# Score products inside the chunks of two gated scans: four places of the TensorE array and a PSUM bank per head

## Chip, cores, metric

The kernel runs on one core of one Trainium2 chip. The metric is the device time of one execution in microseconds. The kernel before was run three times: 878.19, 876.57 and 876.63 us, median 876.63. The profile comes from an execution of its own, which took 878.09 us; the span that it shows, from the first to the last instruction, is 876.2 us.

## What is computed

One layer of an encoder trunk over 512 positions and 1024 channels: a modulated RMS norm, one projection into all branches, three token mixers in parallel (differential attention with 4 heads, the HGRN2 scan with 4 heads of 64 channels, the GLA scan with 4 heads of 32 key channels), a gated merge, an output projection, and an MLP. The change concerns the two scans. Both run forwards and backwards with their own decays, and both are this recurrence:

```python
def chunk_scan(q, k, v, log_a):
    """Gated linear recurrence S_t = diag(a_t) S_{t-1} + k_t v_t^T, o_t = S_t^T q_t, in chunkwise form."""
    ...
        diff = cum[:, :, :, None, :] - cum[:, :, None, :, :]
        decay = jnp.where(causal_in_chunk, jnp.exp(jnp.where(causal_in_chunk, diff, 0.0)), 0.0)
        scores = jnp.einsum('bhtk,bhsk,bhtsk->bhts', qc, kc, decay)
        o_intra = jnp.einsum('bhts,bhsv->bhtv', scores, vc)
```

`scores` inside a chunk is what the change touches: for every pair of positions of a chunk a product over channels whose decay depends on the pair.

## The kernel before

**Order of the program.** An opening reads the input and the first weights and multiplies a first slab of projections. Then come three scans: H0 and H1 (two heads of HGRN2 each, 64 rows of the array a head) and G (the four GLA heads, 32 rows each). Then attention in four heads of four query tiles, the merge, the output projection and the MLP. The other projections (tiles named `tp`, `aq`, `ak`, `gb`, `gc`, `up` and so on) are written as generators in a queue. `pump(n)` takes n steps of the queue and is called inside the scans and in attention, so that projection products stand between the products of the scans. Below, such a product is called a filler. A filler 512 columns wide is one step of L218 to L220, one 256 columns wide (`tp`) one of L388 to L390.

**The order on the engines** is not the order of the code. The tile framework plays the program through ahead of time and orders each engine's instructions by code position and readiness, tile buffers included: an instruction stands later if the buffer that it writes is not yet free. On the chip each engine then runs its list in that order and waits where an operand or a buffer is late.

**A scan** (`scan_tile`). A chunk tile holds 128 positions, and four of them (c = 0 to 3) make 512. Scores are built level by level, for block sizes B = 64, 32, 16, 8, 4, 2, 1 and last 0 (the diagonal). For each level VectorE (DVE) makes the two operands `ea` and `eb` (subtractions L541, L542, products with q and k L545, L547), ScalarE (ACT) takes their exponentials (L543, L544), and `level_scores` multiplies them on TensorE (PE, L629) and moves the results out of PSUM: level 64 with ACT copies into the score tile `SC` (L635), level 32 with an ACT copy into the packed tile `PK` (L637), every other level with a masked DVE copy into `PK` (`copy_predicated`, L639). After the last level `PK` is copied into `SC` (L559).

**A batch** is one call of the loop in `level_scores`: two heads, four chunk tiles, two blocks of 64 keys, so 16 products of 64 by 64, in float32. The trace shows two matmul records for each, so 32 a batch. H0 and H1 have one batch a level, G has two (names `h0` and `h2`): 8 + 8 + 16 = 32 batches. Before, the two heads of a batch write into one bank, head 0 on partitions 0 to 63 and head 1 on 64 to 127, so that the products take two places of the array in turn:

```python
T.matmul(p4[64 * h:64 * h + 64, c, b, :], eb[rr, s0:s0 + 64], ea[rr, t0:t0 + 64], start=True, stop=True)
```

**PSUM.** Eight banks in three pools: `ps_mm` (3 banks, projections), `ps_lv` (3 banks, scores and attention), `ps_ms` (2 banks). `ps_ms` also serves the end of each scan: the transposed keys `kt` (L583), the chunk states `kv` (L590), the output `o` (L612, L614), and then the head norm's mean square `ms` (L647). The output bank is given back when the head norm on DVE (L649, tile `Hn1sq` for scan H1) has read it; that instruction needs the reciprocal root `Hn1rsl` (ACT, L175 and L176) of `Hn1ms`.

**Exponent buffers.** The `ea` and `eb` tiles of a scan come from a pool of six, so three levels can be alive: the operands of level 8 go into the buffers of level 64 and wait until every product of level 64 is done.

**Modulation tiles.** `ada_tile` (L162) multiplies and sums a 128 x 1024 tile on DVE. Eight of them (`ada16` to `ada23`) belong to the first merge steps in the queue.

## Time and profile before

| | |
|---|---|
| three runs, median | 876.63 us |
| the profiled execution | 878.09 us |
| its span | 876.2 us |
| PE busy | 858.6 us (98%) |
| DVE busy | 608.5 us (69%) |
| ACT busy | 439.0 us (50%) |
| PE's share of the chain that ended last | 94% |
| the 32 score batches of the scans | 82.5 to 207.4 us |

A busy PE here is a PE that always has a product in flight; it is not a PE at its peak. Whether a stage is limited by PE is therefore read from the starts of the products, not from the busy share. The share of DVE is a mean over stages: it is nearly always busy in the scans and little in the MLP.

### The profile page before, as it was taken

To read this page: it belongs to the slowest core of one execution; us is meant where nothing else is said; L and a number is where in the kernel's file an instruction comes from. 1 tells how busy PE (TensorE), PEld (TensorE's weight loads), DVE (VectorE), ACT (ScalarE), POOL (GpSimd) and SP (SyncE) were. 2 spreads that over 40 slices of the span, in tenths; PEclk is the share of its full clock that TensorE was granted. 3 is DMA by queue.
4 is the path that set the end of the run, shared out by engine and by line. 5 is a ranking of instruction groups with operands and counts; after the bars stand their busy time and mean duration, and the time that the engine had idled before them with its cause. 6 is when DMAs were issued, how large, how long until landed. Compare 5 with 4: busy or idle time off the path is not lost.

```text
span 876.2 us, 14164 instructions
## 1 busy us (share of the span) xinstructions
PE 858.6 (98%) x5680; PEld 722.5 (82%) x5680; DVE 608.5 (69%) x1087; ACT 439.0 (50%) x800; POOL 25.1 (3%) x33
## 2 busy tenths in 40 slices
PE   6999999999999999999999999999999999999995
PEld 3797888888777676777778899999998889999885
DVE  7968899595677677856166658766676666776445
ACT  5577887554363544545345446834444433443423
POOL 3700000000000000000000000000000000000000
PEclk9999999999999999999999999999999999999998
DMA  9933111111626454643134501322233233332302
GB/s 347 393 101 120 50 49 50 50 61 57 218 89 203 132 180 133 229 155 121 61 99 142 168 26 51 112 103 97 97 97 97 97 109 102 119 105 97 97 1 96
DMA packets 32817, 103.16 MB, mean 118 GB/s; under 512 B 3664, under 2 KB 6128, under 8 KB 32752
## 3 DMA queue, kind: packets, MB, share of 16 engines
q1 hardware_dynamic: 32752, 102.26, 34.6%
q8 instruction: 44, 0.72, 0.3%
q14 instruction: 21, 0.17, 0.1%
HBM read 100.15 MB, written 2.10 MB: 117 GB/s over the span
## 4 chain that ended last, share of the span: by engine, by line
PE 94%; DVE 3%; ACT 1%; DMA 1%; issue 0%; SPq 0%; DVEq 0%; ACTq 0%
PE w L218 7%; PE w L219 7%; PE w L220 7%; PE s L809 2%; PE ou L218 2%; PE ou L219 2%; PE ou L220 2%; PE tp L388 2%; PE oa L830 2%; PE tp L389 2%; PE tp L390 1%; PE sl L219 1%; PE sl L220 1%; PE sl L218 1%; PE up L218 1%; PE wt L825 1%
## 5 line engine op out<-in xcount | busy, mean ns | idle before, releaser
L162 DVE CUSTOM_DVE_ANT_0 ada<-ada,cb,col 128x1024 f32<-128x1024 f32 x32 | 41.0, 1283 | 30.1 <-DMA ada<-ada 30.1
L1156 DVE SCALAR_TENSOR_TENSOR x<-w,modc,x 128x512 f32<-128x512 f32 (+1 forms) x35 | 24.6, 702 | 34.9 <-PE w L220 34.9
L816 ACT ACTIVATE e<-e,mx 128x512 f32<-128x512 f32 x32 | 22.9, 718 | 18.3 <-DVE mx L815 18.3
L827 ACT COPY wT<-wt 128x128 f32<-128x128 f32 x64 | 12.3, 279 | 18.0 <-PE wt L825 18.0
L813 DVE CUSTOM_DVE_ANT_0 e<-s,nd 128x512 f32<-128x512 f32 x32 | 20.8, 684 | 0.0
L162 DVE CUSTOM_DVE_ANT_0 ada<-ada,cps,col 128x1024 f32<-128x1024 f32 x16 | 19.9, 1271 | 0.9 <-ACT cb L308 0.9
L1119 DVE SCALAR_TENSOR_TENSOR r<-r 128x512 f32<-128x512 f32 x24 | 16.5, 689 | 0.4
L830 PE MATMUL oa<-wT,av 128*128 128x512 f32 x32 | 14.4, 592 | 0.0
L928 DVE SCALAR_TENSOR_TENSOR x<-ou,modc,x 128x256 f32<-128x256 f32 (+1 forms) x12 | 6.8, 571 | 8.9 <-PE ou L220 8.9
L822 DVE SCALAR_TENSOR_TENSOR e<-e,mx,e 128x512 f32<-128x512 f32 x16 | 12.0, 748 | 0.3
L882 DVE SCALAR_TENSOR_TENSOR gas<-gas,upa 128x512 f32<-128x512 f32 x8 | 5.4, 685 | 9.3 <-PE upa L220 9.3
L349 ACT ACTIVATE hf<-hf,modc,amix 128x512 f32<-128x512 f32 x7 | 5.7, 816 | 11.6 <-DVE modc L162 8.0
L830 PEld LDWEIGHTS oa<-wT,av 128*128 128x128 f32 x32 | 6.1, 190 | 6.1 <-issue 5.5
L825 PEld LDWEIGHTS wt<-ident,e 128*128 128x128 f32 x64 | 7.7, 140 | 3.1 <-issue 0.7
L825 PE MATMUL wt<-ident,e 128*128 128x128 f32 x64 | 9.8, 276 | 0.0
L322 POOL TENSOR_TENSOR hf<-x,rx 128x512 f32<-128x512 f32 x7 | 9.5, 1356 | 0.0
L885 ACT ACTIVATE mgh<-part 128x512 fp32r<-128x512 f32 x8 | 5.0, 633 | 7.2 <-DVE part L883 7.2
L649 DVE SCALAR_TENSOR_TENSOR An3sq<-oa,gsub,An3rsl 128x512 f32<-128x512 f32 x1 | 0.8, 751 | 10.9 <-ACT An3rsl L176 10.9
L649 DVE SCALAR_TENSOR_TENSOR Hn1sq<-H1o,col,Hn1rsl 128x512 f32<-128x512 f32 x1 | 0.8, 751 | 10.8 <-ACT Hn1rsl L176 10.8
L821 DVE TENSOR_SCALAR e<-e,mx 128x512 f32<-128x512 f32 x16 | 7.7, 479 | 0.0
L543 ACT ACTIVATE Gea<-Gea 128x512 f32<-128x512 f32 x7 | 4.4, 627 | 4.2 <-PE Gl4h L629 3.3
L886 DVE SCALAR_TENSOR_TENSOR mgl<-part,mgh 128x512 fp32r<-128x512 f32 x8 | 5.4, 688 | 1.5 <-ACT mgh L885 1.4
(7290 smaller groups left out, 3351.8 us busy)
## 6 DMA issues: line engine op xcount, KB each, us to landing
ada<-ada SPq DMA_DIRECT2D x48, 512.0 KB, 4.3
x<-xT SPq DMA_DIRECT2D x16, 256.0 KB, 4.3
outT<-o SPq DMA_DIRECT2D x8, 256.0 KB, 2.2
w10r<-w SPq DMA_DIRECT2D x2, 512.0 KB, 6.3
w11r<-w SPq DMA_DIRECT2D x2, 512.0 KB, 5.1
w12r<-w SPq DMA_DIRECT2D x2, 512.0 KB, 3.3
w13r<-w SPq DMA_DIRECT2D x2, 512.0 KB, 4.0
w14r<-w SPq DMA_DIRECT2D x2, 512.0 KB, 3.1
```

The costliest lines, as they stand in the source:

```text
L162: V.tensor_tensor_reduce(w, w, c_, scale=1.0, scalar=C("ada_b", ADA_BLK[u]), op0=ALU.mult, op1=ALU.add, accum_out=o)
L218: T.matmul(ps, wh, xh, start=first, stop=False)
L219: T.matmul(ps, wh, xl, start=False, stop=False)
L220: T.matmul(ps, wl, xh, start=False, stop=last)
L388: T.matmul(o, hh, wh, start=k == 0, stop=False)
L389: T.matmul(o, hh, wl, start=False, stop=False)
L809: T.matmul(sc[i], q_[rr, qs], k_[rr, :], start=n_ == 0, stop=n_ == 2)
L813: V.tensor_tensor_reduce(s_, sc[i], nd[:, 384 - P * qt:896 - P * qt], scale=slope, scalar=-3e38, op0=ALU.add, op1=ALU.max, accum_out=mx[:, ...
L816: A.activation(s_, s_, AF.Exp, bias=mx[:, 2 + i:3 + i], accum_out=mx[:, 4 + i:5 + i])
L825: T.transpose(ps[:, k * P:(k + 1) * P], e[0][:, k * P:(k + 1) * P], ident)
L830: T.matmul(o, av[k][:, hd * P:(hd + 1) * P], wT[k], start=k == 0, stop=k == 3)
L1156: V.scalar_tensor_tensor(x, self.ps[:, sl], modc[:, 40 + self.m:41 + self.m], x, ALU.mult, ALU.add)
```

## The change

Each head gets a bank of its own: head 0 of a batch from `ps_lv`, head 1 from `ps_ms`, 256 columns of each. The partition half now tells the block of keys (b), not the head. In turn, the 16 products take four places of the array: two row groups (the heads) by two column groups (the blocks). The number of products, and the number of copies at level 64 and at the end, stays. The copy at level 32 and the masked copy at the other levels become two, each half as wide, one per head: 4 more on ACT and 24 more on DVE.

```diff
         for h in range(nh):
-            pk = PK[h // 2].rearrange("p (c b t) -> p c b t", c=4, b=2)[64 * (h % 2):64 * (h % 2) + 64]
+            pk = PK[h // 2].rearrange("p (h c t) -> p h c t", h=2, c=4)
             for b in range(2):
                 bb = slice(64 * b, 64 * b + 64)
-                A.copy(c3(SC[h])[bb, :, bb], pk[:, :, b, :])
+                A.copy(c3(SC[h])[bb, :, bb], pk[bb, h % 2])
...
         for h0 in range(0, len(rows), 2):
             pump(npump)
-            ps = ps_lv(f"{n}l{B}h{h0}")
-            p4 = ps.rearrange("p (c b t) -> p c b t", c=4, b=2)
+            ps = [pool(f"{n}l{B}h{h0 + h}")[:, 0:256] for h, pool in enumerate((ps_lv, ps_ms))]
+            p3 = [t.rearrange("p (c t) -> p c t", c=4) for t in ps]
             for c in range(4):
                 for b in range(2):
                     s0, t0 = c * P + 64 * b, c * P + 64 * (b if li else 1 - b)
                     for h in range(2):
                         rr = slice(rows[h0 + h], rows[h0 + h] + step)
-                        T.matmul(p4[64 * h:64 * h + 64, c, b, :], eb[rr, s0:s0 + 64], ea[rr, t0:t0 + 64], start=True,
+                        T.matmul(p3[h][64 * b:64 * b + 64, c, :], eb[rr, s0:s0 + 64], ea[rr, t0:t0 + 64], start=True,
                                  stop=True)
-            if li == 0:
-                for h in range(2):
+            for h in range(2):
+                pk = PK[h0 // 2][:, 256 * h:256 * h + 256]
+                if li == 0:
                     for b in range(2):
                         bb, o = slice(64 * b, 64 * b + 64), 64 * (1 - b)
-                        A.copy(c3(SC[h0 + h])[bb, :, o:o + 64], p4[64 * h:64 * h + 64, :, b, :])
-            elif li == 1:
-                A.copy(PK[h0 // 2], ps)
-            else:
-                V.copy_predicated(PK[h0 // 2].rearrange("p (n t) -> p n t", n=8),
-                                  masks[:, li - 2, :].unsqueeze(1).to_broadcast([P, 8, 64]),
-                                  ps.rearrange("p (n t) -> p n t", n=8))
+                        A.copy(c3(SC[h0 + h])[bb, :, o:o + 64], p3[h][bb])
+                elif li == 1:
+                    A.copy(pk, ps[h])
+                else:
+                    V.copy_predicated(pk.rearrange("p (c t) -> p c t", c=4),
+                                      masks[:, li - 2, :].unsqueeze(1).to_broadcast([P, 4, 64]), p3[h])
```

Since the order on the engines follows buffers and readiness, the change also moves instructions. Three places show how. In the names, `H1l4h0` is scan H1, level 4, head 0 (before: the batch that begins with head 0); the number behind an underscore is the buffer.

First, PE in scan H1 at levels 4 and 2. Before, a batch is one name with 16 products:

```order
L629 MATMUL H1l8h0_1560<-H1ea8_1548,H1eb8_1549 64x64 x16
L629 MATMUL H1l4h0_1585<-H1ea4_1578,H1eb4_1579 64x64 x6
L647 MATMUL Hn0ms_1394<-Hn0sq_1392,blk64_117 128x512
L629 MATMUL H1l4h0_1585<-H1ea4_1578,H1eb4_1579 64x64 x10
L629 MATMUL H1l2h0_1610<-H1ea2_1603,H1eb2_1604 64x64 x16
L388 MATMUL tp20_1778<-wt20h_1768,h2h_329 128x256
```

Now the end of level 4, the whole of level 2, and a filler:

```order
L630 MATMUL H1l4h0_1607<-H1ea4_1600,H1eb4_1601 64x64
L630 MATMUL H1l4h1_1608<-H1ea4_1600,H1eb4_1601 64x64
L630 MATMUL H1l2h0_1634<-H1ea2_1627,H1eb2_1628 64x64 x7
L630 MATMUL H1l2h1_1635<-H1ea2_1627,H1eb2_1628 64x64 x7
L630 MATMUL H1l2h0_1634<-H1ea2_1627,H1eb2_1628 64x64
L630 MATMUL H1l2h1_1635<-H1ea2_1627,H1eb2_1628 64x64
L390 MATMUL tp30_2008<-wt31h_2004,h7l_502 128x256
```

At level 4 the heads take turns; at level 2 seven products of head 0 stand ahead of seven of head 1, and one pair takes turns.

Second, PE in scan G around level 4. Before, nine fillers stand between two batches:

```order
L629 MATMUL Gl4h0_2200<-Gea4_2168,Geb4_2169 64x64 x16
L218 MATMUL aq0p_2196<-h1h_291,aq0h_2192 128x512
L219 MATMUL aq0p_2196<-h1l_292,aq0h_2192 128x512
L220 MATMUL aq0p_2196<-h1h_291,aq0l_2193 128x512
L218 MATMUL aq0p_2196<-h2h_329,aq0h_2192 128x512
L219 MATMUL aq0p_2196<-h2l_330,aq0h_2192 128x512
L220 MATMUL aq0p_2196<-h2h_329,aq0l_2193 128x512
L218 MATMUL aq0p_2196<-h3h_367,aq0h_2192 128x512
L219 MATMUL aq0p_2196<-h3l_368,aq0h_2192 128x512
L220 MATMUL aq0p_2196<-h3h_367,aq0l_2193 128x512
L629 MATMUL Gl4h2_2227<-Gea4_2168,Geb4_2169 64x64 x16
```

Now, from level 8 to level 2, no filler stands between:

```order
L630 MATMUL Gl8h1_2155<-Gea8_2125,Geb8_2126 64x64 x8
L630 MATMUL Gl8h3_2193<-Gea8_2125,Geb8_2126 64x64 x8
L630 MATMUL Gl4h0_2244<-Gea4_2212,Geb4_2213 64x64 x8
L630 MATMUL Gl4h2_2273<-Gea4_2212,Geb4_2213 64x64 x8
L630 MATMUL Gl2h0_2310<-Gea2_2293,Geb2_2294 64x64
L630 MATMUL Gl4h1_2245<-Gea4_2212,Geb4_2213 64x64 x8
L630 MATMUL Gl4h3_2274<-Gea4_2212,Geb4_2213 64x64 x8
L630 MATMUL Gl2h0_2310<-Gea2_2293,Geb2_2294 64x64 x7
L630 MATMUL Gl2h2_2350<-Gea2_2293,Geb2_2294 64x64 x8
L219 MATMUL gc0p_2672<-h1l_292,gc0h_2668 128x512
```

The heads stand one after the other, and the fillers that were between the batches (`aq0`) now stand ahead of scan G.

Third, DVE from the head norm of scan H1 on. Before, the operands of level 4 of scan G follow it:

```order
L649 SCALAR_TENSOR_TENSOR Hn1sq_1730<-H1o1_1715,col_128,Hn1rsl_1734 128x512
L651 SCALAR_TENSOR_TENSOR Hn1sq_1730<-Hn1sq_1730,bg1s_830 128x512
L541 TENSOR_TENSOR Gea4_2168<-glz_1747 128x2x64x4
L542 TENSOR_TENSOR Geb4_2169<-glz_1747 128x2x64x4
L183 TENSOR_TENSOR Hn1ol_1740<-Hn1sq_1730,Hn1oh_1739 128x512
L639 COPY_PREDICATED Gpk0_1819<-masks_546,Gl16h0_2031 128x512
L545 TENSOR_TENSOR Gea4_2168<-Gea4_2168,cqv_1128 128x512
L547 TENSOR_TENSOR Geb4_2169<-Geb4_2169,ckv_1070 128x512
```

Now it is level 8, with modulation tiles between:

```order
L650 SCALAR_TENSOR_TENSOR Hn1sq_1760<-H1o1_1745,col_128,Hn1rsl_1764 128x512
L162 ISA ada16_2905,modc_157<-ada16_2905,cb_156,col_128 128x1024
L162 ISA modc_157 128x1
L652 SCALAR_TENSOR_TENSOR Hn1sq_1760<-Hn1sq_1760,bg1s_830 128x512
L214 TENSOR_TENSOR ubc0l_2780<-ubc0r_2777,ubc0h_2779 128x512
L183 TENSOR_TENSOR k1l_2630<-ak1p_2604,k1h_2629 128x512
L183 TENSOR_TENSOR Hn1ol_1770<-Hn1sq_1760,Hn1oh_1769 128x512
L541 TENSOR_TENSOR Gea8_2125<-glz_1777 128x2x32x8
L542 TENSOR_TENSOR Geb8_2126<-glz_1777 128x2x32x8
L162 ISA ada17_2908,modc_157<-ada17_2908,cb_156,col_128 128x1024
```

All eight modulation tiles `ada16` to `ada23` now stand on DVE between the head norm and level 0 of scan G; before, they stood behind scan G.

## Rows read from the trace of the kernel before

**Rows 1.** The page: busy time of PE; the chain that ended last.

```profile
PE 858.6 (98%) x5680; PEld 722.5 (82%) x5680; DVE 608.5 (69%) x1087; ACT 439.0 (50%) x800; POOL 25.1 (3%) x33
...
PE 94%; DVE 3%; ACT 1%; DMA 1%; issue 0%; SPq 0%; DVEq 0%; ACTq 0%
```

**Rows 2.** Busy time by stretch: length, then each engine; PEclk, DMA last.

```profile
120.00:140.00 20.00, 20.00 (x206) 17.23 (x204) 19.93 (x33) 18.26 (x35) 0.00 (x0) 1.00 0.33 106
...
195.00:210.00 15.00, 15.00 (x176) 11.87 (x175) 7.04 (x11) 5.74 (x12) 0.00 (x0) 1.00 0.19 71
```

**Rows 3.** Timeline of PE, scan H0: start, length, engine, line, tiles, records.

```profile
83.52 1.10 PE L629 MATMUL H0l32h<-H0ea,H0eb 64*64 64x64 f32 x32
84.45 0.75 PE L629 MATMUL H0l16h<-H0ea,H0eb 64*64 64x64 f32 x20
```

**Rows 4.** Timeline of PE, scan G: two batches on different row groups meet.

```profile
175.56 0.27 PE L629 MATMUL Gl16h<-Gea,Geb 32*64 32x64 f32 x2
175.60 0.28 PE L629 MATMUL Gl32h<-Gea,Geb 32*64 32x64 f32 x3
...
175.73 0.22 PE L629 MATMUL Gl32h<-Gea,Geb 32*64 32x64 f32 x1
```

**Rows 5.** Timeline of PE: 512-wide fillers around a batch of scan G.

```profile
189.08 0.40 PE L220 MATMUL aq0p<-h6h,aq0l 128*128 128x512 f32 x1
...
190.81 0.39 PE L219 MATMUL aq0p<-h7l,aq0h 128*128 128x512 f32 x1
191.04 0.40 PE L220 MATMUL aq0p<-h7h,aq0l 128*128 128x512 f32 x1
```

**Rows 6.** Timeline of PE: 256-wide fillers, first and last of 35.

```profile
170.56 0.27 PE L388 MATMUL tp<-wt31h,h5h 128*128 128x256 f32 x1
...
174.59 0.28 PE L390 MATMUL tp<-wt30h,h1l 128*128 128x256 f32 x1
```

**Rows 7.** Timeline, head norm of scan H1: PE, ACT, DVE.

```profile
169.58 1.02 PE L647 MATMUL Hn1ms<-Hn1sq,blk 128*128 128x512 f32 x2
...
174.26 0.63 ACT L176 ACTIVATE Hn1rsl<-Hn1rsl 128x512 f32<-128x512 f32 x1
...
174.92 0.75 DVE L649 SCALAR_TENSOR_TENSOR Hn1sq<-H1o,col,Hn1rsl 128x512 f32<-128x512 f32 x1 [10.84 <-ACT Hn1rsl L176]
```

**Rows 8.** Timeline of PE: first instruction behind scan G's last batch.

```profile
207.29 0.55 PE L583 MATMUL Gkt<-ident,Gkft 128*128 128x128 f32 x3
```

**Rows 9.** Timeline of DVE, scan G: a lo part, operands, a masked copy.

```profile
184.10 1.22 DVE L214 TENSOR_TENSOR aq1l<-aq1r,aq1h 128x1024 fp32r<-128x1024 f32 x1
185.24 1.34 DVE L639 COPY_PREDICATED Gpk<-masks,Gl8h 128x512 f32<-128x512 uint8 x2
186.46 0.69 DVE L541 TENSOR_TENSOR Gea<-glz 128x512 f32<-128x512 f32 x1
187.06 0.70 DVE L542 TENSOR_TENSOR Geb<-glz 128x512 f32<-128x512 f32 x1
```

**Rows 10.** Timeline of DVE: two instructions 384 wide.

```profile
195.35 0.54 DVE L572 TENSOR_TENSOR Gkbt<-Gkbt,ckv 128x384 f32<-128x384 f32 x1
195.81 0.55 DVE L572 TENSOR_TENSOR Gqft<-Gqft,cqv 128x384 f32<-128x384 f32 x1
```

**Rows 11.** Timeline of DVE: a modulation tile.

```profile
215.80 1.28 DVE L162 CUSTOM_DVE_ANT_0 ada<-ada,cb,col 128x1024 f32<-128x1024 f32 x1 [0.60 <-DMA ada<-ada]
217.01 0.08 DVE L162 DVE_READ_ACCUMULATOR2_ANT modc<- 128x1 f32 x1
```

**Rows 12.** Timeline, scan H1: first operands on DVE, first batch on PE.

```profile
127.55 1.89 DVE L545 TENSOR_TENSOR H1ea<-H1ea,hgq 128x512 f32<-128x512 f32 x3
...
130.78 1.15 PE L629 MATMUL H1l64h<-H1ea,H1eb 64*64 64x64 f32 x32
```

**Rows 13.** Busy time by stretch, as rows 2: the opening.

```profile
20.00:24.00 4.00, 1.10 (x4) 0.66 (x4) 3.77 (x7) 2.16 (x3) 1.64 (x2) 1.00 1.02 406
24.00:30.00 6.00, 6.00 (x20) 4.72 (x20) 5.93 (x11) 3.62 (x6) 5.54 (x4) 0.72 1.03 405
```

## The prediction

> **What bounds the kernel now.** I read the page first: PE is in flight for 98% of the span and holds 94% of the chain that ended last [rows 1]. So time leaves only through PE, and comes back as soon as PE waits. Next the stretches of the scans: PE never stands idle there, but DVE is just as full in scans H0 and H1 (19.93 of 20 us) and gets slack only late in scan G (7.04 of 15 us) [rows 2]. The scans are thus near the point where DVE decides. Then the starts of single products on the timeline, since a busy PE says nothing about its pace.
>
> **The pace of a batch.** A batch of scan H0 starts at 83.52 and the next at 84.45: 0.93 us for 32 records, that is 0.0583 us for each two records, one at each of the two places [rows 3]. A place is thus held for 0.0583 us, and in that time the array does nothing elsewhere. Would four places run side by side? The trace has one spot: where batch `Gl32h2` (heads 2 and 3) meets `Gl16h0` (heads 0 and 1, other row groups, other bank), the first records of the new batch start at 175.56, while records of the old one still start up to 175.73 [rows 4]. There both pairs of row groups advance together. So I take four places at full pace. Each pair of products (head 0, head 1) that takes turns then costs 0.0583 us instead of 0.1167.
>
> The Trainium skill ("TensorE: Matmul & The Clock Gate", section "Wait — 56ns, not 53.3ns?") speaks against that: starts of matmuls are never closer than about 25 ns. By that a batch takes 32 x 25 ns = 0.80 us, an estimate from that page, and saves 0.13 us instead of 0.47. In this trace records start closer at the meeting just named, so I go by the trace.
>
> **How many pairs take turns.** A full set of 32 batches would save 32 x 0.467 = 14.9 us. The order does not give that. Head 1 waits for a bank of `ps_ms`, of which there are two, and where that bank is late the list puts head 1 behind head 0, as at H1l2 in the order shown. Eight products of one head still use two places (the two blocks of keys) and cost what they did. Counting the new order: 56 pairs in H0 (7 of 8 batches), 33 in H1, 23 of 128 in G. That is 112 x 0.0583 = 6.5 us, of which 5.2 in H0 and H1.
>
> **Meetings and changes of mode.** Where head blocks on different row groups follow each other, they overlap. At the meeting above this gave 0.17 us (175.73 less 175.56) [rows 4]. The new order has about 22 more such meetings, 21 of them in G: 3.5 us. Every stretch of score products between fillers costs a drain and an uncovered weight load on either side: from 189.08 to 190.81 is 1.73 us, less two fillers at 0.233, less 0.93 for the batch, leaves 0.33 us [rows 3, 5]. The new order has 19 stretches where there were 26: 2.3 us. Together PE could gain 6.5 + 3.5 + 2.3 = 12.3 us, if it never waited.
>
> **What the bank costs: scan G is tied to the end of scan H1.** `ps_ms` also holds H1's `kt`, `kv`, `o` and `ms`. So heads 1 and 3 of level 64 in G wait, in the new order, until `Hn1ms` has been made and read. The operands of level 8 need the buffers of level 64, so DVE cannot begin level 8 until then. Before, level 8 was ready at that moment and DVE began level 4 (the third place in the section on the change). Meanwhile PE takes fillers, and those are used up when G's levels come.
>
> First, when `Hn1ms` ends. Before: 170.6 [rows 7]. The new order has 54 more 256-wide fillers ahead of it, at (174.59 - 170.56)/34 = 0.118 [rows 6], and 81 more 512-wide ones at 0.233 [rows 5]: 6.4 + 18.9 = 25.3 us; 24 fewer products of G (1.4); 5.2 us less for the pairs; 0.9 for a meeting and two stretches. 170.6 + 25.3 - 1.4 - 5.2 - 0.9 = 188.4 if PE does not wait in H1.
>
> It does wait. H1's first operands end on DVE at about 128.2, the batch begins at 130.78, and PE will be 1.7 us earlier; but the new list puts about 2.7 us of other DVE work ahead of them: PE waits 1.9 us [rows 12]. Scan H1's second heads wait for `Hn0ms` in the same way; from `Hn0ms` on, about 3.1 us on ACT (before, the two root steps of `Hn1rsl` with what stood between took 4.3 [rows 7]; fewer copies stand between now) and 13.9 us on DVE's list lead to the operands of level 8, against 14.7 us of fillers, scores and changes of mode on PE: a wait of 2.3 us. Head 1 of level 2 waits 1.5 us for the masked copy of level 8, H1's `kt` 0.6 us for that of level 1. Together 6.3 us, with ends at 2 (the first wait alone) and 9 (half as much again): `Hn1ms` ends at 194.7.
>
> Then DVE sets the end of G. Its list from `Hn1sq` to the last masked copy: 8 modulation tiles at 1.25 (1.21 to the next start, and the read) [rows 11] = 10.0; 24 half copies; 21 instructions 512 wide at 0.60 [rows 9] = 12.6; six 384 wide at 0.46 [rows 10] = 2.8; `gb1l` 1.14 [rows 9]; the first step 0.8 [rows 7]. A half copy is not in the trace: between 0.31 (half of the 0.61 from start to start) and 0.61 (no cheaper) [rows 9]. I take 0.36: from 512 to 384 wide a plain instruction falls from 0.60 to 0.46 [rows 9, 10], so 256 fewer elements take off about 0.25. 24 x 0.36 = 8.6. Sum 36.0 us. Ahead of the list stand the two root steps on ACT with two copies between them where there were eight: 4.3 us before [rows 7], 2.3 us now. G ends at 194.7 + 2.3 + 36.0 = 233.0.
>
> PE has in these 38 us: 50 fillers (11.7), 232 products, 8.6 us with their pairs and meetings, six changes of mode (2.0): 22.3. It waits 16 us, spread over the levels. G's part of the 12.3 us gained is lost in that wait.
>
> Before, G ended at 207.3 [rows 8]. The new order has done 65 more 512-wide fillers by then, 15.2 us: the same work was done at 222.5. **So the new kernel is 10.5 us behind at the end of G.** After that PE decides again and the lists are alike, except for the first head of attention: 54 fewer fillers stand between its first and fifth score tile (90 for 144), while DVE has 10 us less to do there. Its ends are 0 (all covered by the 90) and 54 x 0.233 = 12.6 (each missing filler is a wait). I take 2 us, near the low end, because four tiles with 90 fillers still have over 21 us of fillers on PE.
>
> Sum: 878.1 + 10.5 + 2 = 890.6 for a profiled execution; that one stood 1.46 us above the median of the runs. **889 us.**
>
> The other edits have one answer: the four more level-32 copies on ACT lie beside products (ACT is half idle [rows 1]), and cost ACT's fixed part each if that cover is gone, under 1 us in all; SP's list is the same.
>
> **Rivals.**
> 1. *The gain arrives.* If DVE works through G's levels early enough, because its list holds less than I add up (the modulation tiles come behind the levels in effect, or half copies overlap), PE keeps all of it: 876.6 - 12.3 = 864. For it: DVE had slack in the late part of G [rows 2]. Against: an engine's list is fixed, and the tiles stand in it. Chance 0.10. With most waits small the time would be within 0.2%: 0.07.
> 2. *The places do not run four at a time*, so the change does not do what it says: two row groups in one column group take turns. Then the 5.2 us of H0 and H1 do not come; 1.9 of them were a wait for DVE anyway: 889 + 3.3 = 892. For it: no row shows it over a whole batch. Against: [rows 4]. Chance 0.10. By the skill's limit on starts, above, it would be 889 + 2 = 891.
> 3. *The clock falls.* The granted clock was 0.72 of full speed from 24 to 30 us, right after a stretch with PE busy for 1.10 of 4 us [rows 13], so a part of it ran at 1.2 instead of 2.4 GHz. If the waits in G bring that about, PE's 22.3 us there become up to 44.6, which is 6.6 more than DVE's 38: 895. Against: PE's waits in G are 1 to 3 us each with products between. Chance 0.06.
>
> **How the numbers follow.** The forecast (slower, DVE decides in G) has 0.67; rivals 2 and 3 are slower as well; so slower 0.83, same 0.07, faster 0.10, where 0.2% is about what a measurement of this kernel can tell from no change. The low end: H1's waits at 2 (-4.3), attention at 0 (-2), half copies at 0.31 (-1.2), and about 3 us if the levels' waits close up, 878, and 877 to take in a part of the cases within 0.2%. The high end: attention near its upper end (+10.6), 900. Range 877 to 900.
>
> **What would show it.** Right: `Hn1ms` ending near 195, the last `Gl0h` near 233, DVE without gaps between, PE with gaps of 1 to 3 us at `Gl8h` to `Gl1h` that end with a DVE instruction; batches of H0 starting 0.47 us apart instead of 0.93. Wrong: `Gl0h` ending before 224, or DVE with gaps in G; for rival 2, H0 batches still 0.9 us long; for rival 3, a granted clock under 1 between 195 and 233. The forecast falls if half copies or modulation tiles on DVE are much cheaper than their neighbours.

## The result, and the profile after

The changed kernel takes 901.40 us (median of 4 runs, 899.68 to 905.68), against 876.67 for the kernel before beside it: 1.0285 times, with an interval of 1.0261 to 1.0309. The forecast had the direction and most of the mechanism, but not the size: 24.7 us lost where 12.5 were predicted, just outside the range. The profiled execution (905.68 us) is the slowest of the four, and its span is 27.6 us above that of before; the account below is of that execution, so its sum is about 3 us above what the median lost.

The page of the changed kernel: span, busy time of PE, its granted clock in 40 slices, and the chain that ended last. These lines answer to [rows 1].

```profile
span 903.8 us, 14219 instructions
...
PE 867.1 (96%) x5680; PEld 726.4 (80%) x5680; DVE 608.5 (67%) x1111; ACT 447.3 (49%) x810; POOL 25.1 (3%) x33
...
PEclk9999999997797999999999999999999999999998
...
PE 85%; DVE 8%; ACT 3%; DMA 2%; issue 1%; SPq 0%; DVEq 0%; ACTq 0%
```

PE held 94% of the chain before and holds 85% now; DVE has 8% instead of 3%. Each digit of the clock line stands for 22.6 us; the kernel before has no dip in that place.

The waits of PE, whole program, longest first (us in all, times, longest). In the kernel before none of these from H0 to attention was there:

```profile
PE up L218 <- ACT Gn0oh L182: 5.3, 1, 5.3
PE Gl2h L630 <- DVE Geb L547: 3.3, 1, 3.3
...
PE Gl1h L630 <- DVE Gpk L641: 2.1, 2, 1.4
PE tp L389 <- DVE wt31l L214: 1.9, 1, 1.9
PE H1l2h L630 <- DVE H1pk L641: 1.4, 1, 1.4
...
PE Gl8h L630 <- DVE Geb L547: 1.0, 1, 1.0
...
PE H0kt L583 <- DVE H0pk L641: 0.9, 1, 0.9
```

From 80 to 300 us the gaps of PE over 0.15 us sum to 20.1 us. The table by stretch (length, busy time of PE, weight loads, DVE, ACT, POOL, then the granted clock) shows what goes with them; it answers to [rows 2]:

```profile
210.00:220.00 10.00, 6.85 (x103) 5.03 (x98) 10.00 (x20) 5.20 (x7) 0.00 (x0) 0.76 0.33 103
220.00:230.00 10.00, 8.32 (x119) 6.76 (x119) 8.74 (x17) 1.89 (x4) 0.00 (x0) 0.56 0.56 183
230.00:240.00 10.00, 7.50 (x124) 6.18 (x125) 6.82 (x19) 4.48 (x12) 0.00 (x0) 0.61 0.19 55
...
265.00:275.00 10.00, 4.36 (x15) 1.87 (x16) 2.49 (x4) 7.47 (x9) 0.00 (x0) 0.91 0.00 1
275.00:285.00 10.00, 10.00 (x26) 6.97 (x25) 5.87 (x17) 4.77 (x9) 0.00 (x0) 0.58 0.00 0
```

In G, DVE is full where PE is emptiest (210 to 220 us), which is what "DVE decides in G" means. Ahead of attention (265 to 275 us) both have room, and ACT is the busiest. And after the waits PE runs at 1.2 instead of 2.4 GHz for a part of the time: in all 37.5 us between 80 and 300 us, in stretches from 164.0, 211.8, 218.6, 232.2 and 273.2 us on. In 32.8 of them PE had products in flight; the rest were waits. The kernel before has none there.

The timeline of PE in scan H0 (start, length, line, tiles, records) answers to [rows 3]:

```profile
82.56 0.69 PE L630 MATMUL H0l64h<-H0ea,H0eb 64*64 64x64 f32 x32
83.07 0.65 PE L630 MATMUL H0l32h<-H0ea,H0eb 64*64 64x64 f32 x32
83.54 0.64 PE L630 MATMUL H0l16h<-H0ea,H0eb 64*64 64x64 f32 x16
```

Batches start 0.51 and 0.47 us apart where they started 0.93 us apart: four places work at full pace. The same timeline at the end of H1, the end of G, and ahead of attention answers to [rows 7, 8]:

```profile
196.36 1.02 PE L648 MATMUL Hn1ms<-Hn1sq,blk 128*128 128x512 f32 x2
...
233.86 1.79 PE L630 MATMUL Gl0h<-cqv,Gks 32*64 32x64 f32 x58 [0.41 <-DVE Gpk L641]
...
268.09 1.13 PE L648 MATMUL Gn1ms<-Gn1sq,blk 128*128 128x512 f32 x2 [0.38 <-ACT Gn1sq L646]
274.48 0.79 PE L218 MATMUL up<-Gn0oh,ubc0h 128*128 128x512 f32 x1 [5.26 <-ACT Gn0oh L182]
```

`Hn1ms` ends at 197.4 us and the last product of `Gl0h` at 235.65 us, called G's end here.

**Where the 27.6 us arise.** Over PE's records I summed the time that each product takes in the kernel before, and compared the moments at which both kernels had done equal work. How far the changed kernel is behind (negative is ahead):

| at us of the changed kernel | 115 | 155 | 170 | 205 | 235 | 265 | 290 | 480 |
|---|---|---|---|---|---|---|---|---|
| behind, us | -2.1 | 0.9 | 2.7 | 0.1 | 13.0 | 16.4 | 26.6 | 27.3 |

Other ways of weighing equal work move single entries by up to 1 us or so. So almost nothing net up to 205 us, 13 us in scan G, 3.4 between G and attention, 10.2 in the first head of attention, and under 1 afterwards.

### The profile page after: what moved, and what is told of

Same layout as the page of the kernel before. It is cut to its first block, busy times and chain, and to the rows that moved or that the text cites. A ratio compares the mean times of both kernels' runs of the same rounds, so it can differ in the third digit from the quotient of the medians.

```text
span 903.8 us, 14219 instructions
## 1 busy us (share of the span) xinstructions
PE 867.1 (96%) x5680; PEld 726.4 (80%) x5680; DVE 608.5 (67%) x1111; ACT 447.3 (49%) x810; POOL 25.1 (3%) x33
## 4 chain that ended last, share of the span: by engine, by line
PE 85%; DVE 8%; ACT 3%; DMA 2%; issue 1%; SPq 0%; DVEq 0%; ACTq 0%
PE w L218 7%; PE w L219 7%; PE w L220 7%; PE s L810 2%; PE ou L220 2%; PE ou L218 2%; PE ou L219 2%; PE oa L831 2%; PE sl L219 1%; PE sl L220 1%; DMA ada<-ada 1%; PE sl L218 1%; DVE ada L162 1%; PE up L218 1%; PE up L219 1%
## 5 line engine op out<-in xcount | busy, mean ns | idle before, releaser
L828 ACT COPY wT<-wt 128x128 f32<-128x128 f32 x64 | 12.3, 281 | 16.3 <-PE wt L826 16.3
L630 PE MATMUL Gl2h<-Gea,Geb 32*64 32x64 f32 x64 | 4.0, 303 | 4.2 <-DVE Geb L547 3.3
```

The lines of the kernel that those rows point to most:

```text
L828: A.copy(wT[k][:, qs], ps[:, k * P:(k + 1) * P])
```

## The experiments

All times of the experiments in one table. Waits are PE's gaps over 0.15 us from 80 to 300 us, "low" is the time at 1.2 GHz in the same stretch. The last three columns count from the start of `H0l64h` in the same trace, since the opening varies by up to 1.9 us from one execution to the next. `Gl0h` depends on how many fillers the order puts ahead of it; `ou`, the output projection behind attention, has the same work ahead of it in every kernel, apart from products on zeros in e6, e9 and e11. The traces are of one execution each; the medians are of 4 to 11.

| kernel | median us | ratio to before, interval | waits | low | H0 ends | `Gl0h` ends | `ou` starts |
|---|---|---|---|---|---|---|---|
| before | 876.67 | 1 | 0.0 | 0.0 | 34.3 | 124.8 | 391.5 |
| changed | 901.40 | 1.0261 to 1.0309 | 20.1 | 37.5 | 32.0 | 153.1 | 419.0 |
| e1 | 893.58 | 1.0170 to 1.0232 | 15.7 | 17.1 | 34.0 | 139.5 | 406.1 |
| e2 | 901.07 | 1.0259 to 1.0297 | 13.7 | 37.5 | 36.7 | 165.0 | 417.2 |
| e3 | 880.55 | 1.0025 to 1.0063 | 4.0 | 6.8 | 32.0 | 126.9 | 393.5 |
| e4 | 900.62 | 1.0248 to 1.0299 | 12.4 | 27.3 | 33.5 | 145.3 | 413.4 |
| e5 | 902.34 | 1.0265 to 1.0302 | 14.8 | 37.5 | 34.9 | 154.0 | 417.3 |
| e6 | 898.74 | 1.0227 to 1.0267 | 8.5 | 10.2 | 32.0 | 151.5 | 413.8 |
| e7 | 881.15 | 1.0029 to 1.0059 | 2.9 | 13.7 | 34.3 | 127.9 | 394.5 |
| e8 | 882.21 | 1.0034 to 1.0073 | 8.7 | 17.1 | 32.0 | 130.9 | 397.5 |
| e9 | 880.07 | 1.0019 to 1.0039 | 2.3 | 3.4 | 34.3 | 128.3 | 394.9 |
| e10 | 880.07 | 1.0016 to 1.0046 | 2.6 | 0.0 | 34.3 | 126.9 | 393.5 |
| e11 | 899.75 | 1.0243 to 1.0271 | 13.7 | 30.7 | 32.0 | 153.4 | 415.0 |
| e12 | 882.74 | 1.0044 to 1.0078 | 2.4 | 6.8 | 34.3 | 129.5 | 396.1 |
| e13 | 883.76 | 1.0054 to 1.0089 | 3.3 | 6.8 | 34.3 | 133.2 | 397.4 |

### Tie or places: e2, e1, e5

e2 makes only the tie: the kernel before, with its one bank a batch taken from `ps_ms`. Two places, whole copies.

```diff
-            ps = ps_lv(f"{n}l{B}h{h0}")
+            ps = ps_ms(f"{n}l{B}h{h0}")
```

> The kernel before with its score bank taken from ps_ms instead of ps_lv; two places, one bank a batch, whole copies. Theory A (the tie by the bank): the tie is there, in every batch, without any of the gain; the order has all fillers up to attention used up before the last levels of scan G. 900 to 930. Theory B (half copies) and theory C (four places): neither is there, so 876.6 within 1%.

Measured: 901.07 us, as theory A had it: the changed kernel's time without its half copies and its four places. Its waits of PE from 100 to 300 us begin with

```profile
PE up L218 <- ACT Gn0oh L182: 5.3, 1, 5.3
PE Gkv L590 <- ACT GkT L585: 2.3, 1, 2.3
PE Gl4h L629 <- DVE Gpk L639: 2.2, 1, 2.2
```

the first of which is the same to a tenth. So taking the banks from `ps_ms` is enough for a loss of this size, and half copies are not needed for it. That the two times agree to 0.3 us is in part chance: e2 ties both heads and not one, leaves a batch two banks instead of three, and by equal work is 8.5 us behind at G's end, where the changed kernel is 12.9 behind, both counted from the start of `H0l64h`; it loses more behind G. Tie and number of banks are not told apart.

e1 takes the tie away: the odd head's bank comes from the pool of the projections.

```diff
-            ps = [pool(f"{n}l{B}h{h0 + h}")[:, 0:256] for h, pool in enumerate((ps_lv, ps_ms))]
+            ps = [pool(f"{n}l{B}h{h0 + h}")[:, 0:256] for h, pool in enumerate((ps_lv, ps_mm))]
```

> The changed kernel, but the bank of the second head comes from the projections' pool (ps_mm, three banks) and not from ps_ms. Nothing else is edited; the 24 more half copies on DVE stay. Theory A (the bank ties a scan's scores to the end of the scan before, PE uses up its fillers and waits): the tie is gone. The order has 173 pairs of products that take turns (173 x 0.0583 = 10.1 us less) and 35 stretches of scores where the kernel before had 26 (9 x 0.33 = 3.0 us more), and the same fillers ahead of level 0 of scan G as before: 876.6 - 7.1 = 869.5, within 866 to 874, granted clock near 1. Theory B (the half copies on DVE make the scans longer): nothing of the cause is gone, about 895 to 902. Theory C (four places at once cost the array more than they save): more pairs than in the changed kernel, so slower than 901.

Measured: 893.58 (four runs from 891.1 to 896.3); theory A missed, and the time fits B and C no better. The waits in G are gone but for 0.3 us, as A said, and others came earlier:

```profile
PE H1kt L583 <- ACT H1kft L570: 8.2, 1, 8.2
PE H0kv L590 <- ACT H0kT L585: 4.8, 1, 4.8
```

Score banks and projections now share three banks, the order is dealt anew, and at the end of H0 and H1 PE stands idle while ACT works. "Without this tie the gain arrives" was too simple: every pool has somebody else in it.

e5 keeps the tie and takes the four places away: within a batch, all products of the even head come first.

```diff
-            for c in range(4):
-                for b in range(2):
-                    for h in range(2):
+            for h in range(2):
+                for c in range(4):
+                    for b in range(2):
...
```

> The changed kernel with one edit: inside a batch the eight products of the even head come first and then the eight of the odd head, so that no two heads take turns and never more than two places of the array work; banks, copies and pools stay. Theory A (the banks tie the order and make PE wait in scan G and before attention; four places are a real gain, of which only H0's reaches the end): H0's batches last about 1.1 us again, the last Gl0h ends within 4 us of the changed kernel's 235.7, and the time is 3 to 8 us above the changed kernel's 901.4: 904 to 909. Rival B (the four places gain nothing that reaches the end, because all of it falls into waits): 900 to 903. Rival C (heads in turn cost something themselves, on PE or by the clock): below 898.

Measured: 902.34, 0.9 us above the changed kernel; rival B's numbers held, and theory A's did not. H0 alone is 2.96 us longer (34.92 for 31.96), but 1.7 of it is a stretch of 3.4 us at 1.2 GHz, and PE waited 0.2 us less for `glz` there, so heads in turn save about 1.5 us in H0 over heads one after the other. Over the kernel before, the changed kernel saves 3.25 (34.31 less 31.96 and the 0.9 us of the wait for `glz`), just the prediction's 56 x 0.0583 = 3.3; e5 keeps some 1.8 of it. The reason is in its trace: with one head after the other, a head overlaps with the next head at every change, on the other two row groups, and batches start 0.59 us apart instead of 0.93.

```profile
81.09 0.80 PE L630 MATMUL H0l64h<-H0ea,H0eb 64*64 64x64 f32 x26
81.68 0.27 PE L630 MATMUL H0l32h<-H0ea,H0eb 64*64 64x64 f32 x2
```

So the prediction's "Eight products of one head ... cost what they did" does not hold where another head follows; it counted such changes only as meetings between batches.

### One part alone: e3, e7, e8

Each has four places and two banks (`level_four`, the changed loop) in some scans, and the loop of the kernel before (`level_two`) in the others: e3 in H0, e7 in G, e8 in both. The copies out of `PK` go with the loop.

```diff
+    def level_scores(n, *args):
+        (level_four if n == "H0" else level_two)(n, *args)
```

> Four places and a bank per head in scan H0 only, where no scan goes before that could hold a bank; H1 and G as before. Theory A: 56 pairs take turns, 56 x 0.0583 = 3.3 us less, no tie; the order has five fewer stretches of scores (1.7 us less); but H1's first operands on DVE come no earlier, which takes up to 2 us back: 871 to 875. Theory B: six more half copies on DVE in a stretch where DVE is full, 6 x 0.1 = 0.6 us: 877. Theory C: slower than 877.

> Scans H0 and H1 as in the kernel before, scan G with a bank per head and four places (54 pairs in turn by the order). The tie of G's odd heads to the end of H1 is there, but H1 itself is not put off: Hn1ms stands behind 81 us of fillers instead of 103 in the changed kernel (78 before). Theory A (it is the re-dealt order of H1 and G together, not the places, that costs): Hn1ms ends at 171 to 177, the last Gl0h at 203 to 209, PE waits under 3 us in all, and the time is 870 to 876 (54 x 0.058 = 3.1 us from the pairs and up to 3 from meetings, less small waits); if one or two waits of about 1 us bring a stretch at 1.2 GHz, 876 to 882. Rival F (any use of these banks in G makes G wait for H1's end as in the changed kernel): G ends after 220 and the time is 888 to 900.

> Scan H1 as in the kernel before, H0 and G with a bank per head and four places (56 and 60 pairs in turn). Theory A: the gains of the two parts add, 3.4 us in H0 and 3 to 6 in G: 867 to 873 with no wait over 1 us; with waits like those of the run with H0 alone (two of about 1 us at H0kt and H0o and one stretch at 1.2 GHz, 5 to 8 us) 876 to 882. Rival F (G's banks tie it to the end of H1 whatever the order): 885 to 900.

Measured: 880.55, 881.15 and 882.21, all a little slower than before (each interval lies above 1), and the two parts together are no better than either. The gains of theory A did not come in any of the three. e3 shows why most plainly. Its waits from 60 to 300 us:

```profile
PE H0o L615 <- DVE H0S L601: 1.2, 1, 1.2
PE H0kt L586 <- DVE H0pk L669: 0.9, 1, 0.9
PE Gl4h L632 <- DVE Gpk L642: 0.9, 1, 0.9
PE glz L731 <- ACT lr L727: 0.9, 1, 0.9
```

H0 is 2.35 us shorter although PE waits 0.9 us for `glz` in it, so PE's work fell by 3.3 us. The waits for `glz`, `H0kt` and `H0o` take 3.0 of them back, 2.1 for DVE and 0.9 for ACT: at the end of `Hn0ms`, 60.26 us after the start, the kernel is where it was before (60.19). From 120 to 140 us, up to shortly ahead of that, DVE was busy for 19.93 of 20 us before [rows 2]. That e3 is slower, and not only equal, comes later, in G: the wait of 0.9 us at `Gl4h` and 6.8 us at 1.2 GHz behind it. So the places themselves did not cost (theory C), though the time fits its "slower than 877".

In e7, G's odd heads wait for `Hn1ms`, though H1 is not put off. DVE does 0.46 us of work from 160 to 170 us, where it did 4.08 before (the first line is of the kernel before, the others of e7), and lacks that time later:

```profile
160.00:170.00 10.00, 10.00 (x87) 8.53 (x83) 4.08 (x6) 3.11 (x6) 0.00 (x0) 1.00 0.34 107
...
160.00:170.00 10.00, 10.00 (x84) 8.83 (x83) 0.46 (x2) 1.25 (x3) 0.00 (x0) 1.00 0.19 62
...
180.00:190.00 10.00, 8.50 (x210) 6.71 (x208) 9.23 (x19) 4.57 (x9) 0.00 (x0) 0.69 0.02 4
```

Rival F (G after 220 us) did not come: the tie is cheap where the end of H1 is not late. Theory A's 870 to 876 did not come either; its second branch, 876 to 882 after waits and a stretch at 1.2 GHz, did (one wait of 1.4 us and four of 0.3 to 0.7, with 13.7 us at 1.2 GHz).

### DVE's list in G: e4

The changed kernel, with the 32 modulation tiles of the merge given to steps 2 to 7 and not four to each step, so that `ada16` to `ada23` leave scan G.

```diff
-        for u in range(16 + 4 * m, 20 + 4 * m):
+        for u in ((), (), range(16, 22), range(22, 28), range(28, 33), range(33, 38), range(38, 43), range(43, 48))[m]:
```

> The changed kernel with the 32 modulation tiles of the merge given to merge steps 2 to 7 (six or five a step) instead of four to each of 0 to 7, so that none stands on DVE inside scan G. Theory A, as the prediction has it (in G PE waits for DVE's list, 36 us, of which 10.0 are modulation tiles): G ends about 10 us sooner with 3 us fewer fillers done, so 7 us less: 892 to 896, and less of the time at the low clock if the waits are fewer. If G is held up by something else than DVE's list: 900 to 902.

Measured: G ends 7.8 us earlier against the start of H0 (145.25 for 153.10). 14 fewer fillers stand ahead of that point, 3.3 us; by equal work 4.6 us are left, so DVE's list does set a part of G's end. The time, 900.62, does not follow and missed theory A's 892 to 896. From 300 us on PE waits 5.4 us where the changed kernel does not wait at all,

```profile
PE upa L218 <- ACT gas L412: 2.7, 1, 2.7
PE s L810 <- DVE mx L814: 1.9, 1, 1.9
```

and 27.3 us at 1.2 GHz remain. That the moved tiles on DVE cause these waits is likely and not shown.

### What the clock costs: e6, e9, e11

These put products on zeros where PE waits. They are overwritten by the products that follow in the same bank. e6, in the changed kernel's G (12 of 256 columns ahead of each of ten batches); e9, the same in e7 (6 ahead of each of six batches); e11, 14 of 512 columns ahead of the merge product that waited 5.3 us.

```diff
+            if n == "G" and li > 2:
+                for i in range(12):
+                    T.matmul(ps[0], warm[:, 0:P], warm[:, 0:256], start=True, stop=True)
```

> The changed kernel with 12 products of 256 columns on zeros (about 0.11 us each at full clock, so 1.3 us) into the even head's bank ahead of every batch of levels 8 to 0 of scan G, ten batches, 13 us in all; they stand where PE waits for DVE and are overwritten. Theory A (G's end is set by DVE, the low clock of 212 to 242 us is a second cost that the waits bring with them): the granted clock stays at 1 in G, the last Gl0h still ends at 230 to 236, and the time falls only by what the low clock cost PE's own work after G and between the waits, 2 to 8 us: 893 to 899. Rival D (the clock alone makes G long, DVE only waits for slow products): G ends before 226 and the time is below 892. Rival E (the waits cost, the clock nothing): 900 or more, up to 914 if the dummies are not covered by waits.

> The run with four places in G alone (e7, 881.15), with six products of 256 columns on zeros (0.109 us each from start to start in e6, so 0.65 us) ahead of every batch of levels 8, 4 and 2 of G, 36 products, 3.9 us in all; they stand where PE waited for masked copies, the order of the rest is the same up to the end of G. In e7 PE waited 2.9 us there and the granted clock was at 1.2 GHz for 13.6 us from 183.8 on. Theory A' (the waits are small, and it is the low clock after them that turns the gain of G into a loss): no stretch at 1.2 GHz between 180 and 200, the last Gl0h 2 to 6 us earlier against the start of H0l64h than in e7, 875 to 879. Rival (the clock costs nothing here, since DVE sets the pace of these levels anyway): G ends as in e7 or later, 880 to 885.

> The changed kernel with products of 512 columns on zeros ahead of the first product of the merge that waited 5.3 us for Gn0oh: 11 of 14 land there, 2.3 us, and in the order six products of the same merge that do not need Gn0oh now stand there too, 1.4 us; scans H0, H1 and G are unchanged. Theory A' (after a wait the clock falls, and from the end of G on PE decides, so every us at 1.2 GHz there costs half a us): the stretch of 273 to 283 us at 1.2 GHz is gone, which is worth 5 us, and 1.4 us of the wait is used: 893 to 897. Rival (the low clock costs nothing): 899 to 902.

e6: from 200 us on the clock stays at 2.4 GHz until G is over, and G still ends only 1.6 us earlier (151.5 for 153.1), though 17 fewer fillers (4.0 us) stand ahead:

```profile
210.00:220.00 10.00, 8.71 (x158) 6.81 (x157) 10.00 (x21) 2.49 (x4) 0.00 (x0) 1.00 0.34 103
220.00:230.00 10.00, 9.76 (x194) 7.84 (x193) 9.76 (x22) 2.54 (x5) 0.00 (x0) 1.00 0.31 102
```

Rival D, the clock alone, falls. 898.74 us is within theory A's 893 to 899, though a part of the gain may come from the order, which has these fillers behind G and no 5.3 us wait before attention.

e9: the time at 1.2 GHz from 180 to 200 us goes from 13.7 to 3.4 us, and G ends 0.3 us later than in e7. The rival's range (880 to 885) held, mine fell. The 36 products take 3.9 us of PE themselves, so they might have eaten up what the clock gave back; but DVE is busy for 4.00 of 4 us from 184 to 188 us in both traces, so there DVE sets the pace, and PE's clock costs nothing. From 196 us on PE is full in both, up to 197.4 us at 1.2 GHz in both, and e9 says nothing of what the clock costs there.

e11: the stretch at 1.2 GHz behind the wait is gone,

```profile
275.00:285.00 10.00, 10.00 (x44) 6.86 (x42) 6.73 (x18) 6.40 (x12) 0.00 (x0) 1.00 0.00 0
```

and `ou` starts 4.1 us earlier than in the changed kernel (415.0 for 419.0). 1.4 us of that is merge work that now fills the wait. The rest is not the clock's alone: with `Gn1ms` later in PE's list, ACT makes `Gn0oh` ahead of the root steps of `Gn1rsl` and no longer behind them, so that the product that waited starts 1.5 us earlier against the start of H0. The timed median fell by 1.65 us, to 899.75: above the 893 to 897 of theory A', within the rival's 899 to 902. That the low clock counts here is read from the changed kernel itself. There PE does not wait from 274.5 us on, and at 1.2 GHz its 512-wide products start 0.43 us apart, where they start 0.23 apart at 2.4 GHz [rows 5]:

```profile
275.07 0.63 PE L218 MATMUL up<-Hn0oh,ubc1h 128*128 128x512 f32 x1
275.50 0.63 PE L219 MATMUL up<-Hn0ol,ubc1h 128*128 128x512 f32 x1
```

### Can any order keep the gain: e10, e12, e13

Four places in G with the odd head's bank from the projections: e10 with nothing else, e12 with level 64 as before, e13 with ten steps of fillers ahead of G instead of six.

The first pair of lines is e10's edit of e7, the second what e12 adds, the third what e13 adds:

```diff
-            ps = [pool(f"{n}l{B}h{h0 + h}")[:, 0:256] for h, pool in enumerate((ps_lv, ps_ms))]
+            ps = [pool(f"{n}l{B}h{h0 + h}")[:, 0:256] for h, pool in enumerate((ps_lv, ps_mm))]
...
-    def level_scores(n, *args):
-        (level_four if n == "G" else level_two)(n, *args)
+    def level_scores(n, B, *args):
+        (level_four if n == "G" and B != 64 else level_two)(n, B, *args)
...
-N0 = dict(H0=35, H1=0, G=6)
+N0 = dict(H0=35, H1=0, G=10)
```

> Four places in G alone as in e7, with the odd head's bank from ps_mm, the pool of the projections, so that no product of G waits for the end of scan H1; H0 and H1 are those of the kernel before, 60 pairs take turns, and Hn1ms stands behind 73 us of fillers (78 in the kernel before). Theory A (the tie to H1's end, not the four places, makes G wait): no wait over 0.5 us in G, no stretch at 1.2 GHz, Gl0h ends 1 to 5 us earlier against the start of H0l64h than in the kernel before, 871 to 876. Rival (DVE cannot follow G's levels at that pace whatever the banks, since half copies take more of it): waits of 2 us or more for DVE in G with the clock falling after them, 878 to 884. Rival (fillers come late for want of a bank, as in the run with this pool in all three scans): waits for ACT, 882 to 894.

> As e10 (four places in G, the odd head's bank from the projections' pool), but level 64 of G as in the kernel before, so that the order up to the end of H1 is nearly that of the kernel before: Hn1ms stands behind 76.9 us of fillers (78.1 before, 73.1 in e10), 49 pairs take turns. In e10 PE waited 1.2 us for H1S and 1.4 us for the copies of level 64 just before and after Hn1ms, and then gained 1.8 us up to the end of G. Theory A (only those two waits undid e10's gain, and fillers that stand there again cover them): PE waits under 1 us in 150 to 215 us, Gl0h ends 1 to 3 us earlier against the start of H0l64h than in the kernel before, 874 to 876. Rival (the gain in G turns into waits again, since DVE or ACT has no room there either): waits of 1.5 us or more, 877 to 881.

> As e10, with ten instead of six steps of filler work put ahead of scan G's levels in program order, by which Hn1ms stands behind 78.8 us of fillers and the last Gl0h behind 102.6 (99.8 in the kernel before and in e10); 61 pairs take turns. Theory A: with fillers there the two waits of e10 (2.6 us) shrink to under 1 us and the 1.8 us that G gained stays: 874 to 876, if the first head of attention, which has 2.1 us of fillers less in front of it, does not wait. Rival (the gain turns into waits wherever it arises): waits of 1.5 us or more in 150 to 300 us, 877 to 881.

Measured: 880.07, 882.74, 883.76; theory A fell three times, and e12 and e13 lie above their rival's 877 to 881 too. In e10 no product of levels 16 to 0 waits any more, and from 180 us to the end of G the kernel gains 1.8 us; but it went in 3.9 us behind, through

```profile
PE Gl32h L658 <- ACT Gsc L665: 1.4, 1, 1.4
PE H1o L615 <- DVE H1S L601: 1.2, 1, 1.2
```

and through an order with 34 stretches of score products between fillers where there were 26. With other fillers there, the waits are elsewhere. In e12 from 165 to 185 us:

```profile
PE Gl16h L658 <- ACT Gsc L638: 0.8, 1, 0.8
PE Gl16h L658 <- ACT av L780: 0.6, 1, 0.6
PE Gl16h L658 <- ACT Gpk L667: 0.6, 1, 0.6
...
```

With 0.3 us at `Gl32h` these are 2.4 us. Beside them stand 6.8 us at 1.2 GHz, and by the sum over equal work e12 falls back about 6 us there, from 1.8 ahead: the waits, plus half of the slow time. No order that was tried keeps the gain, and no version beats the kernel before. That none exists is not shown.

## Why the prediction was off

**Right:** four places at full pace (0.47 us a batch; the limit on starts that the Trainium skill states in "TensorE: Matmul & The Clock Gate", section "Wait — 56ns, not 53.3ns?", would have made it 0.80, an estimate from that page, and the trace disagrees), the banks of `ps_ms` as the cause (e2), waits on DVE's operands and masked copies in G, and the end of G. Its chain there came out well, in part by luck: `Hn1ms` at 197.4 us for 194.7, then 38.25 us to G's end for 38.3. But the 38.3 ran to the last masked copy, and that one ends at 237.5 us, 40.1 behind `Hn1ms`; the last `Gl0h` does not wait for it. DVE's list in G, in the changed kernel's groups (busy, mean ns of one), and the last masked copies:

```profile
L162 DVE CUSTOM_DVE_ANT_0 ada<-ada,cb,col 128x1024 f32<-128x1024 f32 x8 | 10.2, 1277 | 2.2 <-DMA ada<-ada 2.2
...
L641 DVE COPY_PREDICATED Gpk<-masks,Gl8h 128x256 f32<-128x256 uint8 x4 | 1.5, 430 | 0.0
...
236.05 1.43 DVE L641 COPY_PREDICATED Gpk<-masks,Gl0h 128x256 f32<-128x256 uint8 x4
```

Two half copies in a row take 0.67 us to the next start (at 213.21 us the first, at 213.88 what follows), so 0.34 each where 0.36 was taken; instead, two modulation tiles waited 2.2 us for their DMA, which was not in the sum. Of the 16 us that PE was to wait in G, 7.8 us were waits; the low clock took about 7 more (half of the 14.2 us that PE worked at 1.2 GHz there).

**A sum too low: up to `Hn1ms`.** 6.3 us of waits were foretold there. There are 6.1 us (0.9 at `glz`, 0.9 at `H0kt`, 1.0 for `av`, 1.9 for a weight's low half, 1.4 at `H1l2`), of the right size, but only the last at a place that was named. What the sum did not have is the 3.4 us at 1.2 GHz, worth 1.7. `Hn1ms` came 2.7 us late, and with it G; about 1 us of that stays open.

**The step that failed: "After that PE decides again and the lists are alike, except for the first head of attention ... I take 2 us".** That head costs 10.2 us by equal work: 5.6 in two waits (0.38 and 5.26), and half of the 8.9 us in which PE worked at 1.2 GHz behind them, 4.5. The upper end of 12.6 for uncovered fillers was nearer; the choice near the low end was wrong. The fillers were counted against DVE's work on score tiles, but PE waited for ACT's head norm of G (`Gn0oh`). In the kernel before, fillers (`gb1p`, `gc1p`) cover it; in the changed kernel they had been used up ahead.

**ACT's list had changed too, and neither the prediction nor an experiment looked at it.** An `ACT_TABLE_LOAD`, which loads a set of function tables on ACT, takes 1.28 us in these traces. The head norm's root is a logarithm (L175) and an exponential (L176). In the kernel before, the load of L419 (234.1 us) stands ahead of G's head norms and that of the gate, L412 (246.2), behind them, and none in `Gn0rsl`'s chain:

```profile
236.54 0.69 ACT L175 ACTIVATE Gn0rsl<-Gn0ms,eps 128x512 f32<-128x512 f32 x1 [1.16 <-PE Gn0ms L647]
...
237.60 0.63 ACT L176 ACTIVATE Gn0rsl<-Gn0rsl 128x512 f32<-128x512 f32 x1
240.48 0.62 ACT L182 CAST Gn0oh<-Gn0sq 128x512 fp32r<-128x512 f32 x1 [2.25 <-DVE Gn0sq L651]
```

In the changed kernel the gate's load (251.9) stands between that of L419 (244.5) and the head norms. Three more loads stand between `Gn0ms` and `Gn0oh`, two of them for `Gn1rsl`, whose steps come first in ACT's list:

```profile
268.06 1.28 ACT L176 ACT_TABLE_LOAD   x1
269.35 0.63 ACT L176 ACTIVATE Gn0rsl<-Gn0rsl 128x512 f32<-128x512 f32 x1
270.00 1.28 ACT L175 ACT_TABLE_LOAD   x1
...
272.00 1.28 ACT L176 ACT_TABLE_LOAD   x1
...
273.83 0.60 ACT L182 CAST Gn0oh<-Gn0sq 128x512 fp32r<-128x512 f32 x1
```

DVE has `Gn0sq` ready at 271.5 us. So, as an estimate from these rows, the first load and the 2.3 us from there to the cast are some 3.6 of the 5.3 us that PE waited. In all the changed kernel has 21 loads, the kernel before 15. The kernels with 21 or 23 (changed, e2, e4, e5, e6, e11) take 898.7 to 902.3 us, those with 15 (e3, e7 to e10, e12, e13) 880.1 to 883.8, and e1 with 17 takes 893.6. Loads and a late end of H1 go together in these kernels; no run tells apart what each costs.

**The rival that was priced too low: the clock (0.06, at most 6.6 us, inside G).** The clock did fall, after waits of 1 to 5 us with products between them, which had been taken as a reason against it. Inside G it costs little (e6, e9). From the end of G to 265 us it costs about 3 of the 3.4 us (6.9 us stand at 1.2 GHz, 0.6 of them a wait at `Gkt`), and about 4.5 us in the first head of attention, both outside the stretch in which the rival looked.

Together: 13.0 at the end of G (10.5 predicted), 3.4 (none), 10.2 (2), and under 1 later, against 12.5 in all.

**The gain of 12.3 us** was too high as well. The waits (20.1 us) and half of the 32.8 us worked at 1.2 GHz, less the 27.6 us by which `ou` is later, leave about 9 us by which PE's own work fell, a rough estimate. H0's part was right (3.25 for 3.3); which of the others was too high is not shown. And little of it arrives: nothing was left at `Hn0ms` in e3, and 1.1 us in the changed kernel. Rival 1, for which the gain had to arrive, is refuted in every order tried.

## What to carry to other kernels

Before making the busiest engine faster, ask stage by stage which other engine is nearly as full: here DVE was at 19.93 of 20 us, and nearly each microsecond freed on PE in H0 became a microsecond of waiting, for DVE or for ACT (e3). A bank from another stage's pool is an edge in the program's order and can cost far more than the products that it speeds up, so try the pool alone first, as e2 did. Look at the new list of every engine, ACT's table loads too, and not only at those of PE and DVE. In these traces a wait of PE cost the wait and then, where PE decided behind it, half of the slow-clock time that followed; where DVE decided (e6, e9), the slow clock cost nothing that could be seen.

## What was unexpected of the hardware

- Four places of 64 by 64 in float32, a bank for each row group, hold 32 records in 0.47 us, 15 ns a record. Two heads one after the other already overlap where they change, so that a batch takes 0.59 us instead of 0.93 (e5).
- The granted clock falls to 1.2 GHz after little idleness: in e7 from 183.8 us on, after a gap of 0.27 us between sparse score products and at the start of one of 0.26, with PE busy for 1.50 us from 182 to 184; in e3 after one wait of 0.9 us. In e10, waits of 1.2 and 1.4 us within 10 us, with PE busy for 7.26 of them, brought no fall. What tells these cases apart was not settled.
- 36 products of no use, 0.109 us each, cut the slow time from 13.7 to 3.4 us (e9), and the median by 1.1 us.
- G's head norms cost ACT no table load of their own in the order before and four in the changed one, at 1.28 us each, though the code of the head norm is the same.
